# A constant second operand in PSUM for the scans of stick-breaking attention, two score banks instead of three, carries kept in the scan buffers, fused state and gate operations, reversed operand allocation and transfers in program order, in a one-core hybrid decoder layer

## The chip, the cores and the metric

The kernel runs on one core of one Trainium2 chip. The metric is the time of one launch on the device, in microseconds. The engines are TensorE (PE, its weight loads as PEld), VectorE (DVE), ScalarE (ACT), GpSimd (POOL) and SyncE (SP), which issues nearly all transfers.

## The reference

One decoder layer over 2048 tokens of width 1024, all in float32. The input is normalised and projected once; the columns feed three mixers that run side by side. Their outputs are normalised per head (two of them with a swish gate), joined, projected and added to the input. A SwiGLU feed-forward network of width 2816 with its own norm follows. Cut to what matters here:

```python
z = einsum('bhqd,bhkd->bhqk', qb, kb) * scale
log_keep = where(mask, log_sigmoid(-z), 0.0)
log_rest = cumsum(log_keep, axis=3, reverse=True) - log_keep
weights = exp(where(mask, log_sigmoid(z) + log_rest, -inf))
o_b = einsum('bhqk,bhkd->bhqd', weights, vb)          # stick-breaking attention, 6 heads of 64
state = dec * state + k_to_end.T @ v                  # GLA (4 heads) and HGRN2 (4 heads), per chunk
mixed = concat([rms(o_a) * silu(g), rms(o_b), rms(o_c) * silu(h)])
x = x + mixed @ w_out
gate, up = split(rms_norm(x) @ w_ffn_up)
x = x + (silu(gate) * up) @ w_ffn_down
```

The weight of a key is its sigmoid times the product of (1 - sigmoid) over the keys between it and the query.

## The kernel before

**Number format and products.** Every large product is done in three matmuls of a float32r type: an operand is split into a rounded high part and the remainder as a low part (`conv_w`, L247: a copy on ACT, L248, and a subtraction on POOL or DVE, L249), and high x high, high x low and low x high are summed. The input projection, the up-projection and the down-projection are cut into two by two blocks and done with seven products instead of eight (numbered 1 to 7; sums of blocks are their operands, and each result is added to several output blocks).

**Stages.** The order of the program is: input projection; attention and the two recurrences, interleaved; the output projection, which begins inside the attention; the up-projection; the down-projection. A scheduler puts the instructions of each engine in order from a simulated timeline at build time, as their operands come free there. Where the kernel wants an order of its own it says so: in the attention the class `Chain` ties every PE instruction behind the one written before it, and `tc.keep_in_program_order` ties an instruction behind the one written before it on its engine.

**Attention (`z_step`, L959, to `a_step`, L1010).** Work goes in slots: a unit is a pair of head and key block of 512 for a query group of 512, with four slots (blocks of 128 queries). A slot computes z on PE, one sigmoid of -z into `kp` (L990) and one of z into `w` (L991) on ACT, and then on DVE a running product over `kp`, read backwards (L993, the scan; its second operand is not used, the operation being a bypass, and is given as `kp` again). The last value, the carry, is copied to a small tile by POOL (L996) and is the start of the same block's scan two units later. The product of `w` with the scan's result is made on DVE for one block in four (two in four for the first query group) and on POOL otherwise (L997). Five slots later `w` is transposed on PE (`t_step`), and seven slots later multiplied with the values. The scan's results take turns in a pool of two buffers.

**Recurrences (`decay_levels`, L1050; `hg_chunk`, L1133; `gla_chunk`, L1196).** Between the attention's steps, in the same PE chain, stand steps of the two gated recurrences, in 16 chunks of 128 tokens, two chunks open at a time. A step is a level: POOL and DVE scale queries and keys, PE makes scores into a score tile of one PSUM bank (pool `c_pss`, three banks), and DVE or ACT reads it into a masked matrix (L1075, L1103). A chunk has ten score tiles for HGRN2 and eleven for GLA; the last chunk leaves out two of each. At its end the state is multiplied by the decay on POOL (L1192, L1247) and the new term in PSUM is added on DVE (L1193, L1248).

**Output projection (`Out`, L804).** It takes over the recurrences' PSUM banks when these are done, while the attention goes on. For each of 16 row tiles `load` fetches the mixers' output and the gates, makes 14 squares with sums (one per head, ACT, L826), a reciprocal root in small DVE operations, a scaling of three segments (DVE, L834) and three products with gates and gains (POOL, L836 to L839). `turn` transposes the tile in two halves into a single PSUM bank (pool `d_pt`) and splits them; the steps then run 48 matmuls, the residual, the second norm, and `left`, two more transposes of halves of the row tile before through the same bank. `left_sums` builds the operands of the up-projection and stores them to `xs_s`.

**Up-projection (`up`, L1380; `left_in`, L1369).** The seven left operands of half the tokens stay in SBUF (pool `e_h`, on the right side, 14 tiles of 8 KB per partition, allocated in the order 1, 5, 6, 2, 3, 7, 4, from low addresses to high); they arrive through two staging buffers. The right side held the output weights `woh`, `wol` and `gffn` at its outer end, and the tiles of the output projection below them. Each of 22 column tiles runs seven products, gates the result and stores `h` to `hs_s` (L1418).

**Down-projection (from L1443).** For each of the seven products in the order 1, 2, 5, 6, 3, 7, 4, eight row tiles fill the eight PSUM banks over 11 k-steps of 24 matmuls. A k-step's left operand (`left_dn`, L1460) is made of transfers `ar` and `xa` of `hs_s` (512 KB each, L1454), its right operand (`right_dn`, L1487) of transfers `br` and `xb` of the weights (256 KB each, L1458). `xa` and `xb` of product 5 stay in SBUF and are changed in place for products 6, 3 and 4. `flush_dn` (L1517) adds a product's eight banks to the sums `acc`, which hold the residual; they are fetched in sixteen transfers after the third k-step of the first product (L1558, tied to program order). After products 2, 3, 7 and 4 a quarter of the result is stored (L1544).

## Time and profile before

| | us |
|---|---|
| median of three runs | 3147.08 |
| lowest and highest | 3138.09, 3147.41 |
| profiled execution | 3147.62 |
| its span, first to last instruction | 3145.8 |
| PE busy | 2831.5 |
| DVE busy | 2116.2 |
| POOL busy | 1639.2 |
| ACT busy | 1344.4 |

The profile is one execution of the program. A stage is read in three steps: what share of it each engine is busy (the windows), what PE waited for in it (the waits, summed by who ended them), and then single instructions in order of time (the timeline), where the number in brackets is the idle time of the engine just before, and the name behind it the one that ended it. A busy PE is not a PE at its peak, since the ends of matmuls are modelled: in a steady stretch one of 512 columns starts every 0.23 us, while its own length reads 0.39 us. The granted clock of TensorE is a share of full speed.

### The profile page before, as it was taken

How to read it: one execution, taken by the hardware profiler on the slowest of the kernel's cores; microseconds unless marked ns; L12 is line 12 of the kernel's file. 1: busy time of each engine (PE TensorE's matmuls, PEld its weight loads, DVE VectorE, ACT ScalarE, POOL GpSimd, SP SyncE). 2: the span in 40 equal slices, each digit the busy share in tenths (PEclk: the TensorE clock that was granted, in tenths of full speed). 3: DMA queues.
4: the chain of work that ended last, by engine and by line, in shares of the span. 5: the costliest groups of instructions: out<-in, count | busy, mean ns of one | idle time of the engine just before them, and what ended most of it. 6: DMA issues, size and time to landing. Idle time of an engine off the chain costs nothing. (4 is left out here: it accounts for less than half of the span.)

```text
span 3145.8 us, 43879 instructions
## 1 busy us (share of the span) xinstructions
PE 2831.5 (90%) x14882; PEld 2309.9 (73%) x14882; DVE 2116.2 (67%) x3508; ACT 1344.4 (43%) x2834; POOL 1639.2 (52%) x1640
## 2 busy tenths in 40 slices
PE   5898999997888889878888799999999997899998
PEld 5897878996666666655666588888788885677776
DVE  8886665886888888988866455555755553267443
ACT  5554534453555555566644333333433332323222
POOL 5342554344787887854633244444544442257635
PEclk9999999998889998989988899999999998999999
DMA  3534432536533333123354332222422225564173
GB/s 116 159 108 134 139 127 97 136 94 166 153 104 107 98 100 93 58 94 108 130 173 161 134 114 85 87 87 84 142 87 81 81 81 216 212 234 144 64 241 131
DMA packets 346095, 389.82 MB, mean 124 GB/s; under 512 B 59152, under 2 KB 258064, under 8 KB 344080
## 3 DMA queue, kind: packets, MB, share of 16 engines
q1 hardware_dynamic: 341776, 381.77, 38.4%
q0 software_dynamic: 4096, 5.25, 0.5%
q8 instruction: 119, 1.95, 0.3%
q14 instruction: 104, 0.85, 0.1%
HBM read 278.93 MB, written 108.00 MB: 123 GB/s over the span
## 5 line engine op out<-in xcount | busy, mean ns | idle before, releaser
L1390 PE MATMUL gu<-ah,uh 128*128 128x512 f32 x1232 | 481.3, 391 | 10.1 <-ACT ah L248 10.1
L1391 PE MATMUL gu<-al,uh 128*128 128x512 f32 x1232 | 481.8, 391 | 6.0 <-DVE al L249 5.9
L1392 PE MATMUL gu<-ah,ul 128*128 128x512 f32 x1232 | 481.0, 390 | 0.0
L249 POOL TENSOR_TENSOR ul<-bs,uh 128x512 fp32r<-128x512 f32 x176 | 241.6, 1374 | 243.2 <-ACT uh L248 243.2
L249 POOL TENSOR_TENSOR ul<-us,uh 128x512 fp32r<-128x512 f32 x132 | 176.6, 1339 | 203.6 <-ACT uh L248 203.6
L1390 PEld LDWEIGHTS gu<-ah,uh 128*128 128x128 f32 x1232 | 232.3, 189 | 60.3 <-ACT ah L248 12.0
L1391 PEld LDWEIGHTS gu<-al,uh 128*128 128x128 f32 x1232 | 232.5, 189 | 56.9 <-DVE al L249 8.7
L1552 PE MATMUL dn<-dbh,dah 128*128 128x512 f32 x616 | 224.6, 402 | 48.4 <-ACT dbh L248 41.8
L1392 PEld LDWEIGHTS gu<-ah,ul 128*128 128x128 f32 x1232 | 232.3, 189 | 48.1
L245 DVE TENSOR_TENSOR h<-h,gu 128x512 f32<-128x512 f32 x176 | 120.9, 687 | 205.3 <-PE gu L1392 123.5
L1553 PE MATMUL dn<-dbl,dah 128*128 128x512 f32 x616 | 243.9, 396 | 12.7 <-POOL dbl L249 12.6
L1554 PE MATMUL dn<-dbh,dal 128*128 128x512 f32 x616 | 242.4, 395 | 3.1 <-DVE dal L249 3.0
L248 ACT ACTIVATE uh<-bs 128x512 fp32r<-128x512 f32 x176 | 110.9, 632 | 299.8 <-PE gu L1391 299.6
L993 DVE TENSOR_TENSOR_SCAN pr<-kp,ca 128x513 f32<-128x513 f32 x144 | 213.2, 1484 | 22.0 <-ACT kp L990 17.7
L997 POOL TENSOR_TENSOR w<-w,pr 128x512 f32<-128x512 f32 (+1 forms) x174 | 191.8, 1102 | 46.0 <-DVE pr L993 26.0
L990 ACT ACTIVATE kp<-z 128x512 f32<-128x512 f32 (+1 forms) x240 | 128.0, 533 | 183.4 <-PE z L104 168.7
L104 PE MATMUL z<-sk,sq 128*128 128x512 f32 (+1 forms) x480 | 170.7, 440 | 14.5 <-ACT w L991 8.1
L107 PE MATMUL wt<-ident,w 128*128 128x128 f32 x816 | 147.9, 294 | 39.2 <-POOL w L997 34.3
L1552 PEld LDWEIGHTS dn<-dbh,dah 128*128 128x128 f32 x616 | 118.4, 194 | 80.5 <-ACT dbh L248 49.3
L249 DVE TENSOR_TENSOR dal<-ar,dah 128x1024 fp32r<-128x1024 f32 x44 | 65.0, 1485 | 163.1 <-ACT dah L248 163.0
L248 ACT ACTIVATE uh<-us 128x512 fp32r<-128x512 f32 x132 | 83.1, 631 | 193.0 <-PE gu L1391 130.6
L104 PEld LDWEIGHTS z<-sk,sq 128*128 128x128 f32 x480 | 80.7, 208 | 104.7 <-issue 37.9
(385 smaller groups left out, 7845.1 us busy)
## 6 DMA issues: line engine op xcount, KB each, us to landing
us<-in_w_ffn_up SPq DMA_DIRECT2D x88, 512.0 KB, 3.8
ar<-hs_s SPq DMA_DIRECT2D x88, 512.0 KB, 4.0
hs_s<-h SPq DMA_DIRECT2D x44, 512.0 KB, 2.6
br<-in_w_ffn_down SPq DMA_DIRECT2D x88, 256.0 KB, 3.2
sk<-sk_s SPq DMA_DIRECT2D x60, 256.0 KB, 2.9
st<-xs_s SPq DMA_DIRECT2D x14, 1024.0 KB, 5.2
xt<-in_x SPq DMA_DIRECT2D x24, 512.0 KB, 4.8
sq<-sq_s SPq DMA_DIRECT2D x48, 256.0 KB, 4.8
```

Source lines behind the costliest of these rows:

```text
L104: self._add(nc.tensor.matmul(*a, **k))
L107: self._add(nc.tensor.transpose(*a, **k))
L248: act.activation(wh, st, AF.Copy)
L249: eng.tensor_tensor(wl, st, wh.bitcast(F32), op=ALU.subtract)
L993: dve.tensor_tensor_scan(pr[:, n::-1], kr, kr, 1.0 if u.diag else u.carry[b], op0=ALU.mult, op1=ALU.bypass)
L997: (dve if (b in DVE_B0 if g == 0 else b == DVE_B) else pool).tensor_tensor(w, w, pr[:, 1:n + 1], op=ALU.mult)
L1390: pe.matmul(pv, bh[:, k, :], ah[:, :, k, :], start=(k == 0), stop=False)
L1391: pe.matmul(pv, bh[:, k, :], al[:, :, k, :], start=False, stop=False)
L1392: pe.matmul(pv, bl[:, k, :], ah[:, :, k, :], start=False, stop=(k == KH - 1))
L1552: pe.matmul(pss[i], ah[:, ts_], bh, start=(k == 0), stop=False)
L1553: pe.matmul(pss[i], ah[:, ts_], bl, start=False, stop=False)
L1554: pe.matmul(pss[i], al[:, ts_], bh, start=False, stop=(k == NK - 1))
```

## The change

- **Scan.** `ones`, a column of ones in a PSUM bank of its own, takes the place of the second operand, broadcast along the row, as long as the recurrences run; afterwards the bank goes to the output projection and the scan is given `kp` twice as before. The scores get two banks instead of three.
- **Carries.** Two fixed scan buffers (`prs`, 529 columns) take the place of the pool. Each unit writes one or two columns further right, so that its last value stays untouched until it is read as the start of a later scan. The POOL copies go.
- **States.** The decay product and the add become one fused operation per head (four) or head pair (two) on DVE.
- **Output projection.** One square of the whole row tile on ACT and three reductions on DVE in place of 14 squares with sums; 14 fused products (scale and gate in one) on DVE in place of three on DVE and three on POOL. Once the attention is over, transposes take turns in three PSUM banks instead of one.
- **Up-projection.** The left operands of the first half are allocated in the reverse order, 4, 7, 3, 2, 6, 5, 1.
- **Down-projection.** Every load of `hs_s` and of the weights is tied to program order. The right operand's tiles move to the right side, with a third raw buffer. The order of products becomes 1, 5, 6, 2, 3, 7, 4. After products 5 and 7 both sums are added on DVE straight from PSUM, without the copy on ACT. Two of the three sums of product 6 are put off: two of these POOL adds follow each later k-step.

```diff
@@ class Out
+            self.ptx = None
+        def pt_tile(self, name):
+            return (self.ptx or self.pt).tile([P, KH, P], F32, tag="pt", name=name)
...
+            sq = self.wk.tile([P, D], F32, tag="sq", name=f"msq{t}", bufs=1)
+            act.activation(sq, m, AF.Square)
             for a, b, w, i, j in segs:
-                for h in range(j - i):
-                    sj = self.sm.tile([P, GDV], BF16, tag="sj", name=f"sj{t}_{i}_{h}", bufs=1)
-                    act.activation(sj[:, :w], m[:, a + h * w:a + (h + 1) * w], AF.Square,
-                                   accum_out=ms[:, i + h:i + h + 1])
+                dve.tensor_reduce(ms[:, i:j], sq[:, a:b].rearrange("p (h d) -> p h d", d=w),
+                                  axis=AX.X, op=ALU.add)
...
-                mv = m[:, a:b].rearrange("p (h d) -> p h d", d=w)
-                dve.tensor_tensor(mv, mv, rs[:, i:j].unsqueeze(2).to_broadcast([P, j - i, w]),
-                                  op=ALU.mult)
-            pool.tensor_tensor(m[:, 0:384], m[:, 0:384], gt[:, 0:384], op=ALU.mult)
-            pool.tensor_tensor(m[:, 768:], m[:, 768:], gt[:, 384:], op=ALU.mult)
-            mv = m[:, 384:768].rearrange("p (h d) -> p h d", d=SD)
-            pool.tensor_tensor(mv, mv, gs64.unsqueeze(1).to_broadcast([P, SH, SD]), op=ALU.mult)
+                for n in range(i, j):
+                    cs = slice(a + (n - i) * w, a + (n - i + 1) * w)
+                    g_ = gt[:, cs] if a == 0 else gs64 if a == 384 else \
+                        gt[:, 384 + (n - i) * w:384 + (n - i + 1) * w]
+                    dve.scalar_tensor_tensor(m[:, cs], m[:, cs], rs[:, n:n + 1], g_,
+                                             op0=ALU.mult, op1=ALU.mult)
@@ attention
-        ps_s = open_pool(prc, "c_pss", 3, PSUM)
+        ps_s = open_pool(prc, "c_pss", 2, PSUM)
+        ps_1 = open_pool(prc, "c_ps1", 1, PSUM)
+        ones = [ps_1.tile([P, 512], F32, name="one")[:, 0:1]]
+        dve.memset(ones[0], 1.0)
...
+        prs = [sbk.tile([P, 513 + 16], F32, name=f"pr{i}", bufs=1) for i in range(2)]
...
-                    u.carry = [sbk.tile([P, 1], F32, tag=f"ca{i}", name=f"ca{h}_{g}_{i}", bufs=4)
-                               for i in range(4)]
+                    u.carry = [1.0] * 4
...
-                    u.q, u.carry = p.q, p.carry
+                    u.q, u.carry = p.q, p.last
+                u.last = []
...
-            pr = sbk.tile([P, 513], F32, tag="pr", name=f"pr{h}_{g}_{c}_{b}")
+            at = 4 * (g - c) + 2 * u.j + b // 2
+            pr = prs[b % 2][:, at:at + 513]
...
-            dve.tensor_tensor_scan(pr[:, n::-1], kr, kr, 1.0 if u.diag else u.carry[b],
-                                   op0=ALU.mult, op1=ALU.bypass)
-            if c > 0:
-                pool.tensor_copy(u.carry[b], pr[:, 0:1])
+            dve.tensor_tensor_scan(pr[:, n::-1], kr,
+                                   ones[0].to_broadcast([P, n + 1]) if ones else kr,
+                                   u.carry[b], op0=ALU.mult, op1=ALU.bypass)
+            u.last.append(pr[:, 0:1])
@@ hg_chunk (gla_chunk alike, two operations)
-            pool.tensor_tensor(s_new, s_old, dec.to_broadcast([P, HH, HDV]), op=ALU.mult)
-            dve.tensor_tensor(s_new, s_new, pu, op=ALU.add)
+            for i in range(HH):
+                dve.scalar_tensor_tensor(s_new[:, i, :], s_old[:, i, :], dec[:, i, :], pu[:, i, :],
+                                         op0=ALU.mult, op1=ALU.add)
@@ when the recurrences are done
                 prc.close()
+                ones.clear()
                 out_.open()
@@ after the attention
+    ptx = ExitStack()
+    out_.ptx = open_pool(ptx, "d_px", 3, PSUM)
     for t in outs:
         pass
+    ptx.close()
@@ up-projection
+    ops = {m: tuple(hp.tile([P, 4, KH, P], F32R, tag=f"{x}{m}", name=f"{x}{m}_0")
+                    for x in ("ah", "al")) for m in ORDER[::-1]}
@@ down-projection
+    bop = open_pool(pd, "g_bo", 3, side="right")
...
-        dma.dma_start(t_, hs_s[kh * NK + k][j].rearrange("p i j t -> p (i j t)"))
+        tc.keep_in_program_order(
+            dma.dma_start(t_, hs_s[kh * NK + k][j].rearrange("p i j t -> p (i j t)")))
...
-        dma.dma_start(t_, w_dn[r:r + P, j * 512:j * 512 + 512])
+        tc.keep_in_program_order(dma.dma_start(t_, w_dn[r:r + P, j * 512:j * 512 + 512]))
...
-            t_ = rop.tile([P, 512], F32, tag="br", name=f"br{nm}_{kh}{j}")
+            t_ = bop.tile([P, 512], F32, tag="br", name=f"br{nm}_{kh}{j}")
...
         elif m in (5, 7):
             c = {5: c12, 7: c21}[m]
-            tmp = rop.tile([P, 512], F32, tag="tmp", name=f"tmp{m}_{i}")
-            act.activation(tmp, ps, AF.Copy)
             add(c, c, ps)
-            add(c22, c22, tmp, pool)
+            add(c22, c22, ps)
+            if m == 7:
+                done(8 + i, 1)
         elif m == 6:
             u = held[i]
             add(u, u, ps)
-            add(c12, c12, u, pool)
             add(c21, c21, u)
-            add(c22, c22, u, pool)
+            later.append(lambda: add(c12, c12, u, pool))
+            later.append(lambda: add(c22, c22, u, pool))
...
-    for m in (1, 2, 5, 6, 3, 7, 4):
+    for m in (1, 5, 6, 2, 3, 7, 4):
...
+            for fn in later[:2]:
+                fn()
+            del later[:2]
```

## Rows read from the trace of the kernel before

**Rows 1.** Windows by stage: start and length, busy us and instructions per engine, clock, DMA.

```profile
755.00:1592.00 837.00, 723.44 (x4746) 535.09 (x4747) 700.60 (x1164) 478.20 (x1269) 601.55 (x847) 0.91 0.38 110
1592.00:1785.00 193.00, 148.87 (x642) 116.35 (x641) 112.49 (x316) 72.62 (x267) 59.91 (x51) 0.86 0.48 157
1785.00:2639.00 854.00, 845.50 (x3696) 696.23 (x3696) 509.30 (x594) 293.39 (x463) 409.79 (x302) 0.99 0.29 95
2639.00:3145.80 506.80, 438.27 (x1849) 352.52 (x1848) 240.49 (x187) 136.10 (x179) 251.07 (x153) 0.94 0.53 186
```

**Rows 2.** Waits of PE, 755 to 1592: us in total, times, longest.

```profile
PE wt L107 <- POOL w L997: 34.3, 27, 3.9
...
PE mt L107 <- POOL m L836: 8.8, 1, 8.8
```

**Rows 3.** Groups of the page: count, busy us, mean ns, idle before.

```profile
L993 DVE TENSOR_TENSOR_SCAN pr<-kp,ca 128x513 f32<-128x513 f32 x144 | 213.2, 1484 | 22.0 <-ACT kp L990 17.7 <-POOL w L997 1.7 <-ACT sj L826 1.1
...
L996 POOL COPY ca<-pr 128x1 f32<-128x1 f32 x144 | 45.1, 314 | 85.3 <-DVE pr L993 56.6 <-DVE rfy L84 9.2 <-DVE rmy L84 4.5
```

**Rows 4.** The tile pr: shortest, median and longest in ns.

```profile
L993 DVE TENSOR_TENSOR_SCAN pr<-kp,ca x144: 1247/1286/2356, 856.2 to 1569.7; 128x513 f32<-128x513 f32 x144
...
L997 DVE TENSOR_TENSOR w<-w,pr x66: 267/686/1779, 756.5 to 1558.5; 128x512 f32<-128x512 f32 x36, 128x128 f32<-128x128 f32 x24, 128x384 f32<-128x384 f32 x6
```

**Rows 5.** A group of the page, an add with an operand in PSUM.

```profile
L245 DVE TENSOR_TENSOR h<-h,gu 128x512 f32<-128x512 f32 x176 | 120.9, 687 | 205.3 <-PE gu L1392 123.5 <-issue 81.8
```

**Rows 6.** Waits of PE, 1592 to 1795.

```profile
PE po L902 <- ACT mh L89: 12.9, 9, 4.1
```

**Rows 7.** Windows of line 826 alone, 1592 to 1785: busy us of ACT.

```profile
1592.00:1785.00 193.00, 34.90 (x196) 0.86 0.48 157
```

**Rows 8.** Timeline: start, us, instruction; two score tiles and two readings before them.

```profile
794.00 1.10 PE L104 MATMUL sch<-hq,hk 128*64 128x64 f32 x8
794.84 0.72 DVE L1075 COPY_PREDICATED st_h<-masks,sch 128x256 f32<-128x256 int8 x1
...
1376.64 0.68 PE L104 MATMUL scg<-qx_g,gk 128*128 128x128 f32 x4 [0.97 <-DVE qx_g L1071]
1377.61 0.32 DVE L1248 TENSOR_TENSOR s_g<-s_g,gpu 128x192 f32<-128x192 f32 x1
```

**Rows 9.** Timeline of PE, end of the output projection.

```profile
1768.06 0.39 PE L904 MATMUL po<-woh,ml 128*128 128x512 f32 x1
...
1784.79 0.79 PE L1390 MATMUL gu<-ah,uh 128*128 128x512 f32 x1 [7.53 <-ACT ah L248]
```

**Rows 10.** Timeline of ACT, the same stretch.

```profile
1784.11 4.08 ACT L248 ACTIVATE ah<-st 128x512 fp32r<-128x512 f32 x6 [6.21 <-DMA xs_s<-xs]
```

**Rows 11.** Timeline of PE, start of the down-projection.

```profile
2638.62 0.39 PE L1392 MATMUL gu<-ah,ul 128*128 128x512 f32 x1
2662.54 3.44 PE L1552 MATMUL dn<-dbh,dah 128*128 128x512 f32 x8 [23.53 <-ACT dbh L248]
...
2693.27 3.43 PE L1552 MATMUL dn<-dbh,dah 128*128 128x512 f32 x8 [12.75 <-ACT dbh L248]
```

**Rows 12.** Timeline of SP's queue, the same stretch.

```profile
2641.15 0.32 SPq L1418 DMA_DIRECT2D hs_s<-h  x1
...
2652.19 1.62 SPq L1458 DMA_DIRECT2D br<-in_w_ffn_down  x2
...
2665.94 15.97 SPq L1558 DMA_DIRECT2D acc<-x_s  x16
2682.92 0.33 SPq L1458 DMA_DIRECT2D br<-in_w_ffn_down  x1
```

**Rows 13.** DMA issues of the page: count, KB each, median us to landing.

```profile
ar<-hs_s SPq DMA_DIRECT2D x88, 512.0 KB, 4.0
```

**Rows 14.** Timeline of SP's queue at the turn from product 2 to 5.

```profile
2789.17 1.46 SPq L1454 DMA_DIRECT2D ar<-hs_s  x2
...
2800.80 0.42 SPq L1544 DMA_DIRECT2D out<-acc  x1
```

46 lines of the change are left out of this document (26 added, 20 removed).

## The prediction

> **What bounds the kernel now.** I read the windows by stage first [rows 1]: the 3145.8 us span has five stages, and TensorE (PE) is the engine that should never stand still. In the up-projection (1785 to 2639) it issues 3696 matmuls in 854 us, 0.231 us each, busy 845.5 us: nothing is to be had there. The other stages are not like that. Attention with the recurrences (755 to 1592) leaves PE idle 113.6 of 837 us, the rest of the output projection (1592 to 1785) 44.1 of 193, the down-projection 68.5 of 506.8. Next I read who ends PE's waits. In the attention the first is the product w on POOL, 34.3 us, and one wait of 8.8 us for the first row tile of the output projection [rows 2]. In the tail of the output projection it is the split on ACT, 12.9 us [rows 6], and at its end PE waits 7.5 us more for the first operand of the up-projection [rows 9]. The down-projection loses 23.5 us before its first matmul and 12.8 us three k-steps later [rows 11].
>
> The profiled execution took 3147.62 us, 1.8 us more than its span and 0.5 us from the median of the three runs (3147.08). The sum is made against 3147.6. A difference under 0.3% (9.4 us) is no change here.
>
> **A. Attention, 755 to 1592.** Removed: 144 carry copies on POOL, 45.1 us by their row [rows 3]; two state products per chunk on POOL. The scan of 513 elements has a mean of 1484 ns [rows 3] but a minimum of 1247 and a median of 1286 [rows 4]; the excess sits in a few slow ones (maximum 2356), as if something held them. With the second operand in PSUM I take the minimum: 144 x 0.237 = 34 us of DVE in a stage where DVE is busy 700.6 and POOL 601.6 of 837 us [rows 1]. Scans that run after the recurrences close still take two operands from SBUF, so this is an upper bound, and 0 the lower. That the PSUM operand costs nothing is read from the nearest row: an add of 512 columns with one operand in PSUM takes 687 ns [rows 5], one with both in SBUF a median of 686 [rows 4].
>
> [...]
>
> Added on DVE: six fused state operations per chunk in place of two adds (15 chunks, four more of about 0.27 us, the minimum of a two-operand product [rows 4]: +16 us) and the heavier row-tile preparation, counted in B. So DVE ends about 18 us lighter, POOL over 45 us lighter. PE's waits for POOL should halve (34.3 to 17), and the 8.8 us wait for the first row tile shrinks by 6, since its squares and POOL products are shortened. That is -23, and another -8 for the smaller POOL and DVE waits.
>
> Against it stands the lost third score bank. The trace has 332 score tiles (21 per chunk, 16 chunks, 4 missing at the end). With two banks a tile must wait until the one two before is read out. I compared each tile's start with that moment: 73 start too early for two banks, by 60 us in all; the first and the last [rows 8]: the scores at 794.00 start before the predicated copy at 794.84 is done at 795.56, and those at 1376.64 before the state add is done at 1377.93. What is queued behind such a wait is PE's whole hand-ordered chain: the next z, transposes and products. A lower bound is 0 (DVE reads out faster), an upper 60 or more. I take a quarter, +15, because a delayed PE also delays the tiles behind it, which opens the next gap. A = -23 - 8 + 15 = **-16** (-70 to +45). The carry now stays on DVE, so no scan waits for POOL; the two scan buffers still make each scan wait for the product two slots earlier, as two pool buffers did.
>
> **B. Tail of the output projection.** The 14 squares per row tile keep ACT busy 34.9 us in this stage [rows 7]; one square replaces them. Three reductions and 14 fused products come onto DVE, about 17 x 0.27 = 4.6 us a row tile, and three products each leave DVE and POOL. DVE has room: 112.5 of 193 us [rows 1]. Three transpose banks in place of one let transposes go ahead of the split that empties them. [...]
>
> **C. Start of the up-projection.** The last matmul of the output projection starts at 1768.06, the first of the up-projection at 1784.79 [rows 9]. The operand's conversion on ACT waited for the transfer xs_s out of the staging tile [rows 10]: operand 1 is laid where that tile was. The operands fill 112 KB of the right side and the output weights its outer 68 KB; allocated in reverse, operands 1, 5 and 6 lie over the weights, free with the last matmul. Conversion and subtraction of a quarter cost under 2 us, so the start can be near 1771. The supply of further operands keeps its two staging buffers. **-12** (-16 to 0).
>
> **D. Start of the down-projection.** SP's own rows show the reason for the two stalls [rows 12]: after the last store of h (2641.15) come transfers for later products, the first br issues only at 2652.19, then sixteen acc loads from 2665.94, and the br of the fourth k-step at 2682.92. With program order, ar and br of three k-steps are queued right behind that store, then acc, then the fourth. First matmul: 2641.5 + 4.0 for landing [rows 13] + 0.7 for a conversion (4.08/6 [rows 10]) = 2646.2. Three k-steps of 24 matmuls last 16.6 us, 1.6 more at the slow clock (3.44 us for the first eight [rows 11]): 2664.4. The fourth waits for acc: from its first issue to the restart took 27.3 us (2665.94 to 2693.27); behind six loads, about 2644.5, that gives 2671.8. Before, the fourth started at 2693.27: -21.5. The loads of product 5, which were fetched early, now come within its own stage; I leave 2.5 us for that: **-19** (-25 to -8).
>
> **E. Rest of the down-projection.** The other 32 us of idle time there partly go: POOL's sixteen adds after product 6 are spread over later steps, and the right operand has a third buffer. I take 22 of the 32. But the order has a price. Before, loads of the next product pass the stores of out: ar issued at 2789.17, the first out of that turn at 2800.80 [rows 14]. Now each load is queued behind the last store of the product before, which waits for its add. After products 2 and 3 that is 0.7 (add) + 0.4 (issue) + 4.0 (landing) + 0.7 (conversion) = 5.8 us of empty PE each; after product 7, with two adds per bank on DVE, 8 x 0.69 = 5.5 more: 11.3. Together 23 us. **+1** (-15 to +20).
>
> **Sum.** -16 - 22 - 12 - 19 + 1 = -68: 3147.6 - 68 = 3080 us.
>
> **Rivals.** *Slower: two score banks decide.* Without the 15 us for banks the sum is -83, so from 83/332 = 0.25 us per score tile on, the kernel is slower. If each tile costs 0.35 us (116 us), it takes 3147.6 - 83 + 116 = 3181. For it: PE's order is fixed, and 73 pairs are short already. Against it: 259 are not, and DVE gets lighter. Chance 0.10. *The port is freed in full.* If the slow scans come from POOL reading SBUF at the same time, POOL's operations are held by scans as well, and PE's waits for it go whole: 34.3 and 8.8 [rows 2], twice the 8 us of smaller ones, and nothing for the banks make A -60 and the time 3036. Chance 0.14. [...] The spread of the scan [rows 4] agrees; how much of it reaches PE no row shows. *Order costs more than it gives.* If stores hold the next product's loads at every turn and A gives nothing, D and E cancel: 3147.6 - 22 - 12 = 3114, or 3130 with B at its low end. Chance 0.10. *Nothing reaches the path:* the waits removed are replaced by the next in line, 3147. Chance 0.06.
>
> **Numbers.** The forecast has 0.60 and its own range 3045 to 3115. From 3030 to 3132 all but about 2 in 10 is held: outside lie the slower case, the no-change case and the far end of the freed port (0.10 + 0.06 + 0.03). Faster by over 0.3%: 0.60 + 0.14 + 0.10 = 0.84; within: 0.06; slower: 0.10.
>
> **What would show it.** Right: scans near 1250 ns with little spread until the recurrences end; no carry copies; PE's wait for w about 17 us; up-projection starting some 3 us after the last po; first dn about 5 us after the last store of h; new PE gaps of about 6 us after products 2 and 3 and 11 after 7. Wrong: a scan over 1350 ns with the PSUM operand, score matmuls waiting for predicated copies in most chunks, a first dn behind acc as before, or an idle DVE with PE still waiting for POOL.

## The result and the profile after

| | before | changed |
|---|---|---|
| median of the runs | 3145.18 us (4 runs, 3138.09 to 3147.41) | 3122.27 us (4 runs, 3120.13 to 3129.18) |
| ratio, 95% interval | | 0.9937 (0.992 to 0.9954) |
| profiled execution | 3147.62 us, span 3145.8 | 3122.30 us, span 3120.5 |

The change makes the kernel faster, by 0.6%. That is inside the range of 3030 to 3132 us, but it is 42 us short of the 3080 us forecast: the direction was right, the size a third of what was expected.

The windows by stage of the changed kernel, with the columns of [rows 1]:

```profile
752.00:1579.00 827.00, 718.81 (x4734) 529.65 (x4735) 685.30 (x1345) 448.03 (x1022) 429.94 (x646) 0.92 0.38 111
1579.00:1762.00 183.00, 143.81 (x654) 115.55 (x652) 126.30 (x417) 46.42 (x79) 35.42 (x27) 0.89 0.49 160
1762.00:2622.00 860.00, 848.64 (x3695) 696.41 (x3696) 516.36 (x594) 293.89 (x464) 414.69 (x306) 0.99 0.29 96
2622.00:3120.50 498.50, 435.24 (x1851) 354.67 (x1849) 252.76 (x203) 127.80 (x163) 235.95 (x137) 0.94 0.53 188
```

POOL lost 172 us of work in the attention (601.6 to 429.9) and ACT 26 us in the rest of the output projection (72.6 to 46.4), yet these two stages are only 10 us shorter each. The up-projection is 6 us longer.

For a sharper cut I use the starts of first and last matmuls, which every profile has: the first score product z, the last transpose of w, the last matmul of the output projection (po), the first and last of the up-projection (gu) and of the down-projection (dn). The stretches between them, in us, from starts rounded to 0.1 us (all kernels below are explained in the next section):

| kernel | z to last w | to last po | to first gu | to last gu | to first dn | to last dn |
|---|---|---|---|---|---|---|
| before | 827.1 | 186.2 | 16.7 | 853.8 | 23.9 | 478.7 |
| changed | 819.7 | 181.3 | 9.3 | 860.0 | 3.3 | 490.5 |
| e1 attention undone | 830.2 | 181.5 | 9.3 | 860.5 | 3.3 | 498.6 |
| e2 row tile undone | 819.8 | 164.9 | 9.3 | 861.0 | 3.3 | 493.0 |
| e3 one transpose bank | 810.3 | 190.2 | 10.4 | 859.1 | 3.2 | 491.7 |
| e4 stores later, acc spread | 814.9 | 181.6 | 9.3 | 859.2 | 3.3 | 443.1 |
| e5 products as before | 821.9 | 161.0 | 9.3 | 858.8 | 3.3 | 498.4 |
| e6 stores later | 804.6 | 181.5 | 9.3 | 860.0 | 3.3 | 455.0 |
| e7 old places | 811.5 | 181.0 | 9.3 | 860.2 | 3.3 | 490.1 |
| e8 before, two banks | 838.7 | 183.7 | 16.8 | 855.4 | 24.4 | 479.7 |
| e9 three banks, no constant | 821.1 | 182.3 | 9.3 | 860.3 | 3.2 | 496.3 |
| e10 old places, no square tile | 811.6 | 168.6 | 16.0 | 854.3 | 3.3 | 492.8 |
| e11 e5 and e4 together | 816.1 | 164.3 | 9.3 | 860.4 | 3.3 | 442.0 |
| e12 e11, w on POOL | 829.9 | 163.4 | 9.3 | 862.9 | 3.3 | 444.1 |
| e13 row tiles one earlier | 815.8 | 181.7 | 9.3 | 859.8 | 3.3 | 492.6 |
| e14 e11, adds later | 814.9 | 164.2 | 9.3 | 860.2 | 3.3 | 445.4 |
| e15 e14, first row tile later | 802.0 | 173.8 | 9.5 | 863.2 | 3.3 | 443.3 |
| e16 block sums on DVE | 803.1 | 159.6 | 9.5 | 856.0 | 3.3 | 495.1 |
| e17 all, fused products | 796.2 | 167.8 | 9.4 | 857.5 | 3.3 | 444.9 |
| e18 all, products as before | 803.8 | 159.6 | 9.4 | 859.1 | 3.3 | 445.7 |

The changed kernel, e3, e4, e6 and e7 have the same attention code, and their first column runs from 804.6 to 819.7: one profile tells that stage to some 8 us only. The tail in the second column lies within 1.3 us in the seven kernels that have the changed kernel's output projection (181.0 to 182.3: the changed one, e1, e4, e6, e7, e9, e13). Other kernels with equal tails are up to 3.7 us apart (the kernel before and e8; e2 and e10; e5, e11, e12 and e14). In e15, e17 and e18 the tail holds 516 of the 768 matmuls of the output projection, in all others 498, so the tails of these three compare with each other only.

The scans in the view of the tile pr (duration in ns as min/median/max) did what was forecast:

```profile
L1001 DVE TENSOR_TENSOR_SCAN pr<-kp,pr,one x105: 1243/1271/1283, 845.5 to 1384.2; 128x513 f32<-128x513 f32 x105
L1001 DVE TENSOR_TENSOR_SCAN pr<-kp,pr x39: 1258/1279/2110, 1386.4 to 1555.3; 128x513 f32<-128x513 f32 x39
```

With the constant in PSUM not one of 105 scans takes over 1283 ns; with both operands in SBUF, after the recurrences have closed, the maximum is 2110 again, as it was 2356 before [rows 4]. What the slow ones meet can be counted in the trace, over all scans of 513 elements. With the constant, 106 of 127 run while a POOL instruction runs, and none is slow. With both operands in SBUF, 30 of 41 run with no POOL instruction beside them and none takes over 1289 ns; the other 11 have a median of 2028.

PE's waits for w on POOL fell from 34.3 us [rows 2] to 14.0; the wait for the first row tile is as long as before, only on DVE now. New are waits for the readings of score tiles (st_h, st_g) and for the state operations (s_h, s_g) on DVE. From the view of waits, 752 to 1579 us:

```profile
PE wt L107 <- POOL w L1008: 14.0, 14, 5.5
PE mt L107 <- DVE m L840: 9.3, 1, 9.3
PE ho L104 <- DVE st_h L1086: 8.6, 3, 3.2
PE sch L104 <- DVE s_h L1204: 5.6, 5, 1.7
PE sch L104 <- DVE st_h L1086: 5.2, 5, 1.7
```

The same view of the kernel before, 755 to 1592 us, has two rows that belong beside them, its largest wait for POOL after w and its largest of the new kind:

```profile
PE sch L104 <- POOL hk L1117: 11.5, 10, 5.1
PE go L104 <- DVE st_g L1075: 3.3, 2, 2.0
```

Summed over all such rows from the first z to the last w, PE's waits that POOL ended fell from 71.9 us to 16.3, and those that score readings and state operations on DVE ended rose from 7.8 to 44.0. All waits together fell only from 119.5 to 113.0.

In the tail of the output projection PE now stands still rarely and long, where it stood often and briefly: 12 times for 32.4 us in all, before 26 times for 30.4 us. ACT ended 21.3 us of these waits before and ends 11.5 now; DVE ended 6.2 us and ends 21.0 now. These are single rows of PE's timeline:

```profile
1603.16 0.79 PE L904 MATMUL po<-woh,mh 128*128 128x512 f32 x1 [8.98 <-ACT mh L89]
1643.81 0.80 PE L906 MATMUL po<-woh,ml 128*128 128x512 f32 x1 [4.01 <-DVE ml L90]
1678.61 0.80 PE L904 MATMUL po<-woh,mh 128*128 128x512 f32 x1 [6.35 <-DVE xt L909]
1712.94 0.79 PE L906 MATMUL po<-woh,ml 128*128 128x512 f32 x1 [5.76 <-DVE ml L90]
```

In the down-projection the 23.5 us before the first matmul are gone [rows 11], the stall three k-steps later is not, and three new ones follow products 2, 3 and 7:

```profile
2625.47 2.12 PE L1574 MATMUL dn<-dbh,dah 128*128 128x512 f32 x8 [2.91 <-ACT dbh L248]
2655.40 3.56 PE L1574 MATMUL dn<-dbh,dah 128*128 128x512 f32 x8 [13.21 <-ACT dbh L248]
2906.36 3.78 PE L1574 MATMUL dn<-dbh,dah 128*128 128x512 f32 x8 [8.33 <-ACT dah L248]
2979.10 2.50 PE L1574 MATMUL dn<-dbh,dah 128*128 128x512 f32 x5 [10.37 <-ACT dbh L248]
3054.78 3.55 PE L1574 MATMUL dn<-dbh,dah 128*128 128x512 f32 x8 [13.24 <-ACT dbh L248]
```

SP's own rows (start, duration, issue) show both causes, against [rows 12, 14]: the first loads stand ahead of the last store of h, all sixteen acc loads stand between the third and the fourth k-step, and the loads after product 2 stand behind eight stores of out:

```profile
2611.49 0.32 SPq L1476 DMA_DIRECT2D ar<-hs_s  x1
2614.21 0.33 SPq L1480 DMA_DIRECT2D br<-in_w_ffn_down  x1
2624.70 0.32 SPq L1436 DMA_DIRECT2D hs_s<-h  x1
2626.44 16.04 SPq L1580 DMA_DIRECT2D acc<-x_s  x16
2643.48 0.32 SPq L1476 DMA_DIRECT2D ar<-hs_s  x1
2894.02 5.09 SPq L1541 DMA_DIRECT2D out<-acc  x8
2899.21 0.41 SPq L1476 DMA_DIRECT2D ar<-hs_s  x1
```

### The profile page after: what moved, and what is told of

It is laid out like the page before. It is cut to its first block, busy times and chain, and to the rows that moved or that the text cites. A ratio compares the mean times of both kernels' runs of the same rounds, so it can differ in the third digit from the quotient of the medians.

```text
span 3120.5 us, 43531 instructions
## 1 busy us (share of the span) xinstructions
PE 2817.2 (90%) x14882; PEld 2301.0 (74%) x14882; DVE 2136.6 (68%) x3809; ACT 1280.5 (41%) x2386; POOL 1431.7 (46%) x1402
## 4 chain that ended last, share of the span: by engine, by line
PE 54%; DVE 16%; DMA 7%; issue 5%; POOL 2%; ACT 2%; SPq 1%; DVEq 0%; POOLq 0%; ACTq 0%
PE gu L1409 9%; PE gu L1410 9%; PE gu L1408 9%; PE dn L1574 3%; PE dn L1575 3%; PE dn L1576 3%; PE z L104 2%; PE av L104 2%; DVE pr L1001 2%; PE wt L107 2%; PE sch L104 2%; DMA br<-in_w_ffn_down 2%; DVE m L840 1%; PE scg L104 1%; PE ho L104 1%
## 5 line engine op out<-in xcount | busy, mean ns | idle before, releaser
L1574 PE MATMUL dn<-dbh,dah 128*128 128x512 f32 x616 | 231.3, 404 | 52.2 <-ACT dbh L248 39.7
L1001 DVE TENSOR_TENSOR_SCAN pr<-kp,pr,one 128x513 f32<-128x513 f32 x105 | 133.6, 1273 | 21.0 <-ACT kp L997 20.6
```

What stands on the lines that cost most here:

```text
L1001: dve.tensor_tensor_scan(pr[:, n::-1], kr, ones[0].to_broadcast([P, n + 1]) if ones else kr, u.carry[b], op0=ALU.mult, op1=ALU.bypass)
L1574: pe.matmul(pss[i], ah[:, ts_], bh, start=(k == 0), stop=False)
```

## Experiments

Ratios are to the kernel before, with 95% intervals, timed on the same chip. The changed kernel's is 0.9937.

### Attention: what the constant, the banks and POOL's relief are worth

**e1.** `ps_s` with three banks, `tensor_tensor_scan(pr, kr, kr, ...)`, carry copies and state products on POOL as in the kernel before; the rest is the changed kernel.

> The changed kernel with its attention part undone: both scan operands from SBUF again, three score banks, carry copies and state products on POOL; all other parts of the change stay. In the profile of the changed kernel the stretch from the first score product z to the first matmul of the output projection that has no attention beside it took 827.3 us, against 834.7 us before. Theory 1 (the attention part gives only that: PE's waits for POOL became waits for DVE, which does the state products now): about 3122 + 7 = 3129 us, scans with a mean near 1480 ns again, PE's waits for w on POOL near 34 us. Theory 2 (the DVE work that the attention part added also made the row tiles late, so that the part gives nothing or costs): 3115 to 3122 us, and a shorter tail of the output projection than the 173 us of the changed kernel. Theory 3 (the part gave the 16 us of the forecast and another part took them back): 3138 us.

Measured: 3142.28 us, 0.9975 (0.9963 to 0.9987). By the ratios the part is worth 0.9975 - 0.9937 = 0.4%, 12 us: between theories 1 and 3. The tail stays at 181.5 us, so theory 2 is out.

**e8.** The kernel before with one edit:

```diff
-        ps_s = open_pool(prc, "c_pss", 3, PSUM)
+        ps_s = open_pool(prc, "c_pss", 2, PSUM)
```

> The kernel before with two score banks in place of three and nothing else changed. Theory 1 (a quarter of what the pairs that start too early lack): 15 us slower than the kernel before, ratio 1.005, PE's waits for the predicated copies and the state products on DVE grow by that. Theory 2 (two banks decide): 60 us or more slower, ratio 1.02. Theory 3 (DVE reads out in time whatever the banks): no difference, ratio within 0.002 of 1.

Measured: 3160.91 us, 1.004 (1.0026 to 1.0055), 13 us. Theory 1. PE's waits for score readings and state operations on DVE grow by more than that, from 7.8 to 37.0 us, while its waits for POOL fall from 71.9 to 57.6.

**e9.** The changed kernel with `c_pss` at 3, without `ones`, and the scan reading `kr` twice; carries and fused state products as changed.

> The changed kernel with three score banks and both scan operands from SBUF; the scan buffers that hold the carries, the fused state products and everything else stay. Two banks alone cost the kernel before 0.4% (13 us), and the attention part as a whole gave 0.4% (12 us), so that the rest of the part must give about 25 us. Theory 1 (the constant in PSUM gives most of these 25, because scans no longer meet POOL): without it and with the bank back the time is 5 to 15 us longer than the changed kernel's, ratio 0.996 to 0.998, and the mean of the 513-element scan is back above 1400 ns. Theory 2 (the carry copies and state products taken from POOL give most of them, and the scan's 0.2 us each is hidden): the time is 5 to 12 us shorter, ratio 0.990 to 0.992.

Measured: 3129.52 us, 0.9941 (0.9921 to 0.9962), the changed kernel's ratio within the intervals: neither theory. The long scans are back at a mean of 1421 ns (view of lines, kept apart by shape), and PE's wait for w is 26.0 us:

```profile
L998 DVE TENSOR_TENSOR_SCAN pr<-kp,pr 128x513 f32<-128x513 f32 x144 | 204.4, 1421 | 12.0 <-ACT kp L994 9.7 <-POOL w L1004 2.1
```
```profile
PE wt L107 <- POOL w L1004: 26.0, 25, 5.0
```

So the constant and the bank that it takes cancel, to within the some 8 us that the intervals leave. The waits show both sides: all of PE's waits for POOL are 39.4 us here and 16.3 in the changed kernel, those for score readings and state operations on DVE 7.1 here and 44.0 there. What is left of the part, e1 against e9, 0.0034 or 11 us, goes with the carries and the state products; these two were not parted.

**e12.** e11 (below), with `DVE_B = -1` and `DVE_B0 = (0,)`: nearly all products w on POOL.

> The run before (gate products as before, stores later, acc spread) with the quarter of the products w that DVE does in the attention moved to POOL (of the first group, one of its two). In the changed kernel these 56 products took 40.8 us of DVE up to 1400 us, and POOL was busy 430 of 827 us. Theory 1 (DVE is now what PE waits for in the attention): 5 to 15 us shorter than the run beside it. Theory 2 (a product takes 1.12 us on POOL and 0.73 on DVE and PE waits for w on POOL again): 5 us or more longer.

Measured: 3074.29 us, 0.9762 (0.9749 to 0.9774) against 0.9715 for e11: 15 us longer. The result fits theory 2, its reason doesn't: PE's waits for w on POOL are 17.2 us, 19.0 in e11. PE's busy time grew for the same matmuls, at a lower granted clock (first row e12, second e11; windows from the first z to the last w):

```profile
756.30:1586.20 829.90, 722.14 (x4699) 532.16 (x4700) 663.24 (x1184) 447.93 (x1019) 515.71 (x730) 0.90 0.38 110
```
```profile
750.30:1566.40 816.10, 706.44 (x4701) 519.76 (x4701) 679.47 (x1245) 445.91 (x1019) 462.72 (x672) 0.93 0.39 111
```

Why the clock was granted lower here stays open.

### Output projection: why 22 us became 5

**e2.** Fourteen squares on ACT and products in two steps as before; three transpose banks stay.

> The changed kernel with the preparation of a row tile undone: 14 squares on ACT in place of one, no reductions, three products on DVE and three on POOL in place of fourteen fused ones on DVE; the three transpose banks stay. Theory 1 (the fourteen fused products, 30 us of DVE in the tail, stand in DVE's queue ahead of the adds and splits that PE waits for, and cost about what the one square gives): 3119 to 3125 us; PE's waits in the tail for DVE shrink and those for ACT grow. Theory 2 (the forecast: the squares were what held PE): 3135 us or more, the tail from the first to the last matmul of the output projection 10 us or more longer than 173 us.

Measured: 3110.4 us, 0.9859 (0.9833 to 0.9885): undoing this part makes the kernel 0.8% faster, more than either theory allowed. The tail falls to 164.9 us, with the waits that DVE ends down from 21.0 to 9.8 us.

**e3.** Without `out_.ptx = open_pool(ptx, "d_px", 3, PSUM)`.

> The changed kernel with one transpose bank in the tail of the output projection in place of three. In the profile of the kernel before, PE had 16 waits of 0.7 to 1.2 us in front of transposes in the tail; in that of the changed kernel there are none of them. Theory 1 (the third and second bank removed those): 16 x 0.75 = 12 us slower, 3134 us, and the short waits are back. Theory 2 (the row tiles are late on DVE anyway, so the short waits come out of the long ones): 3122 to 3125 us, short waits back and the waits of 4 to 9 us shorter by as much.

Measured: 3134.4 us, 0.9944 (0.9924 to 0.9964), no difference that the runs can tell; the tail is 190.2 us, 9 longer, as theory 1 has it. Tails together: with one bank 186.2 and 183.7 (row tiles as before: the kernel before, e8) and 190.2 (changed), with three 164.9 and 168.6 (as before: e2, e10) and 181.3 (changed). With row tiles as before the banks alone are worth 15 to 21 us there, nearly all that was forecast for the whole term; the new preparation takes 13 to 16 of them back.

**e5.** Only the fourteen products undone; the one square and the reductions stay:

```diff
-                for n in range(i, j):
...
-                    dve.scalar_tensor_tensor(m[:, cs], m[:, cs], rs[:, n:n + 1], g_, ...)
...
+                dve.tensor_tensor(mv, mv, rs[:, i:j]..., op=ALU.mult)
+            pool.tensor_tensor(m[:, 0:384], m[:, 0:384], gt[:, 0:384], op=ALU.mult)
...
```

> The changed kernel with the fourteen fused products of a row tile undone (three products on DVE and three on POOL, as before), but the one square and its three reductions kept. With squares and products both as before, the ratio to the kernel before was 0.986 against 0.994 with both changed, and the tail from the last transpose of w to the last matmul of the output projection took 164.9 us against 181.3. Theory 1 (the fused products in DVE's queue are the cost): ratio 0.986 or less, the tail 165 us or shorter, because ACT is relieved as well. Theory 2 (the one square with its reductions, a chain from ACT to DVE that ends later than fourteen sums written by ACT alone, is the cost): ratio 0.992 to 0.994, the tail 175 us or more.

Measured: 3107.12 us, 0.9871 (0.985 to 0.9891), tail 161.0 us: theory 1. The square with its reductions is no worse than fourteen squares (164.9). The fused products cost 17 to 20 us of tail (e11, e12 and e14, with the same tail, have 163.4 to 164.3), and the waits that DVE ends fall to 4.0 us without them.

**e13.** To tell DVE's load from the order, the preparation of a row tile was issued one tile earlier (`prep(t + 2)` beside `load(t + 1)`).

> The changed kernel with the preparation of a row tile (loads, square, reductions, the fourteen fused products on DVE) issued one row tile earlier in the program; its work is the same. In the changed kernel the tail from the last transpose of w to the last matmul of the output projection takes 181 us with the fused products and 161 us without them. Theory 1 (not the load on DVE but the place of the products just ahead of the adds and splits that PE waits for): the tail 170 us or less, ratio 0.990 or less. Theory 2 (the load on DVE): the tail 178 us or more, ratio as for the changed kernel, 0.994.

Measured: 3123.27 us, 0.9928 (0.9908 to 0.9948), tail 181.7 us. This reads as theory 2 but is no test: DVE's timeline shows the products at nearly the same places, and PE's five long waits are the same (9.58, 3.54, 4.01, 6.34 and 5.78 us for 8.98, 3.23, 4.01, 6.35 and 5.76). The order on an engine is not that of the program's text where nothing pins it.

What the trace does show is where the products are slow. POOL's and then DVE's timeline of the changed kernel ahead of the 6.35 us wait (start, duration; xn are n in a row):

```profile
1670.58 1.27 POOL L242 TENSOR_TENSOR xs<-xa,xa 128x512 f32<-128x512 f32 x1 [28.75 <-ACT xa L871]
1671.93 1.26 POOL L245 TENSOR_TENSOR xa<-xa,xa 128x512 f32<-128x512 f32 x1
1673.27 1.39 POOL L242 TENSOR_TENSOR xs<-xa,xa 128x512 f32<-128x512 f32 x1
1674.73 1.39 POOL L242 TENSOR_TENSOR xs<-xa,xs 128x512 f32<-128x512 f32 x1
```
```profile
1654.24 0.17 DVE L84 SCALAR_TENSOR_TENSOR rmy<-rma,rmy 128x14 f32<-128x14 f32 x1
1655.08 1.00 DVE L840 SCALAR_TENSOR_TENSOR m<-m,rmy,gt 128x96 f32<-128x96 f32 x4
...
1670.59 1.29 DVE L84 SCALAR_TENSOR_TENSOR rmy<-rma,rmy 128x14 f32<-128x14 f32 x1
1671.91 3.08 DVE L840 SCALAR_TENSOR_TENSOR m<-m,rmy,gt 128x96 f32<-128x96 f32 x4
1674.92 2.26 DVE L840 SCALAR_TENSOR_TENSOR m<-m,rmy,gs 128x64 f32<-128x64 f32 x6
1677.88 0.68 DVE L909 TENSOR_TENSOR xt<-xt,po 128x512 f32<-128x512 f32 x1
```

An operation of 14 columns that takes 0.17 us at 1654 takes 1.29 at 1670, when POOL has just begun a block sum, and it ends with that sum. Four products that take 1.00 us at 1655 take 3.08. The add of po, for which PE waits, stands behind them. This is no single case: of the 224 fused products in the trace 194 run with no POOL instruction beside them and none takes over 0.32 us; the 30 that do run beside one have a median of 1.07 us.

**e16.** The four block sums of every second row tile go to DVE:

```diff
-            sub(s3, a11, a21, pool)
-            add(a21, a21, a22, pool)
-            sub(s2, a21, a11, pool)
-            sub(s4, a12, s2, pool)
+            sub(s3, a11, a21, dve)
...
```

> The changed kernel with the four block sums of every second row tile in the output projection on DVE instead of POOL; the fourteen fused products stay on DVE. Theory 1 (POOL's sums hold the fused products, each for the rest of a POOL instruction): although DVE gets 4 x 0.7 us more per two row tiles, PE's waits of 3.2, 4.0, 6.4 and 5.8 us in the tail shrink and the tail from the last transpose of w to the last matmul of the output projection falls from 181 to 170 us or less; ratio 0.991 or less. Theory 2 (DVE has too much to do or in the wrong order): the tail stays at 181 us or grows; ratio 0.994 or more.

Measured: 3088.93 us, 0.9802 (0.9778 to 0.9826), by the ratios 42 us less than the changed kernel (33 by the medians as they stand); the tail is 159.6 us with DVE no lighter. Theory 1, and more than it asked. Of the gain 22 us lie in the tail. The largest other difference between the two profiles, 16.6 us, is in the attention, which one profile tells to some 8 us only. The waits that DVE ends in the tail fall from 21.0 to 6.2 us. DVE's products fall from means of 382 and 349 ns (changed kernel, 1579 to 1762 us) to 298 and 280 (e16, 1556 to 1720 us), and PE's granted clock in the tail rises from 0.90 to 0.97. The view of lines of the changed kernel and of e16, then the windows of the tail of e16 and of the changed kernel:

```profile
L840 DVE SCALAR_TENSOR_TENSOR m<-m,rmy,gt 128x96 f32<-128x96 f32 (+1 forms) x56 | 18.3, 382 | 0.2
L840 DVE SCALAR_TENSOR_TENSOR m<-m,rmy,gs 128x64 f32<-128x64 f32 x42 | 11.8, 349 | 0.0
```
```profile
L840 DVE SCALAR_TENSOR_TENSOR m<-m,rmy,gt 128x96 f32<-128x96 f32 (+1 forms) x64 | 15.3, 298 | 0.1
L840 DVE SCALAR_TENSOR_TENSOR m<-m,rmy,gs 128x64 f32<-128x64 f32 x48 | 10.5, 280 | 0.0
```
```profile
1556.00:1722.00 166.00, 145.99 (x697) 115.18 (x695) 122.12 (x447) 47.62 (x81) 7.91 (x6) 0.97 0.56 182
```
```profile
1571.60:1753.00 181.40, 148.97 (x681) 118.57 (x679) 123.32 (x405) 44.92 (x77) 34.26 (x26) 0.90 0.50 162
```

The sums themselves are also shorter on DVE, 0.69 us against 1.3; e16 doesn't separate that from the holding. How much DVE is held can be estimated from the traces: for each of its operations that overlaps a POOL instruction in the tail, take its time less the median of the same operation with none beside it (over the kernels here), and sum what is over 0.1 us. That gives 29.7 us on 40 operations in the kernel before, 26.6 on 32 in e5, 20.5 on 21 in the changed kernel and 4.6 on 5 in e16. So the fused products did not make the holding more frequent. They changed what is held: before, 19 of the 40 lay in the preparation of a row tile (norm of the heads and products) and 19 in the second norm; in the changed kernel 20 of the 21 lie in the preparation, like those ahead of the add shown above.

### The start of the up-projection

**e7.** The changed kernel without the reversed `ops`.

> The changed kernel with the operands of the up-projection laid out as before. In the changed kernel the first matmul of the up-projection starts 9.3 us after the last of the output projection (16.7 before), but the stage then takes 860 us (854 before): PE runs at its full rate from 41.3 us after the last matmul of the output projection on, before from 43.7. Theory 1 (the supply of the seven operands through two staging buffers and the conversions on ACT and DVE sets the time, not the first one): the first matmul 7 us later, the last matmul of the up-projection at most 3 us later counted from the last of the output projection. Theory 2 (the early start is a gain of its own): both 7 us later or more.

Measured: 3117.24 us (one run); first gu 9.3 us after the last po, stage 860.2 us: nothing changes, neither theory. The edit that I gave the 12 us is idle here.

**e10.** e7 and e2 together, so also without the 4 KB tile of the squares.

> The changed kernel with the row tile's preparation as before (so without the new buffer of 4 KB for the squares) and the operands of the up-projection laid out as before. Either of the two edits alone left the first matmul of the up-projection 9.3 us after the last of the output projection. Theory 1 (either edit moves the first operand off the staging tile of the last transfer): now the 16.7 us of the kernel before are back. Theory 2 (the gap went with the transpose banks or the earlier row tiles): 9 to 11 us again.

Measured: 3107.33 us (one run), 16.0 us: theory 1. The first gu waits for the operand again:

```profile
1750.74 0.80 PE L1408 MATMUL gu<-ah,uh 128*128 128x512 f32 x1 [7.98 <-ACT ah L248]
```
```profile
1750.06 2.19 ACT L248 ACTIVATE ah<-st 128x512 fp32r<-128x512 f32 x4 [6.66 <-DMA xs_s<-xs]
```
```profile
1757.00 0.80 PE L1407 MATMUL gu<-ah,uh 128*128 128x512 f32 x1 [1.21 <-ACT ah L248]
```

(the first two rows are e10's, the third e7's). In e10 the conversion waits for the transfer out of the staging tile again, as in [rows 10]. So either edit moves the first operand off that tile: the reversed places, or the new tile, which I take to shift the staging tiles by its 4 KB. And it is worth nothing: from the last po to the last gu e10 takes 16.0 + 854.3 = 870.3 us, e2 with the early start 9.3 + 861.0 = 870.3.

### Down-projection: what stands behind the stores

**e4.** Two edits (`done` now only collects the stores, `stores()` issues them):

```diff
-            if m == 1 and k == 2:
-                for t in range(NT):
+            if (m == 1 and k >= 1) or (m == 5 and k < 6):
+                for t in [len(acc)]:
...
+            if k == 2:
+                stores()
```

> The changed kernel with two edits in the down-projection: the stores of out are issued after the loads of the third k-step of the next product instead of ahead of that product's loads, and the sixteen acc loads are issued one per k-step (ten in the first product, six in the second) instead of all sixteen after the third k-step. In the profile of the changed kernel PE stands still 13.2 us before the fourth k-step, 8.3 us after product 2, 10.4 us after product 3 and 13.2 us after product 7, together 45.1 us. Theory 1 (loads queued behind stores and behind acc are the whole of these stalls): 3122 - 45 = 3077 us, at the least 3087 us. Theory 2 (the transfers themselves are the limit, so that the loads would be late in any order): 3110 to 3120 us, with the waits spread over the k-steps.

Measured: 3071.86 us, 0.9747 (0.9726 to 0.9768): theory 1. The first to the last dn takes 443.1 us in place of 490.5, 47.4 less; of the stalls over 3.2 us on PE's timeline only one for POOL is left:

```profile
2830.21 0.80 PE L1583 MATMUL dn<-dbl,dah 128*128 128x512 f32 x1 [6.04 <-POOL dbl L249]
```

**e6.** The stores alone.

> The changed kernel with the stores of out issued after the loads of the third k-step of the next product; the sixteen acc loads stay together after the third k-step. With both edits the down-projection from its first matmul took 444.2 us against 491.6, the ratio was 0.975. Theory 1 (each stall belongs to its own queue): the stalls of 8.3, 10.4 and 13.2 us after products 2, 3 and 7 go and the 13.2 us before the fourth k-step stays: from the first matmul 491.6 - 31.9 = 460 us, the ratio near 0.983. Theory 2 (the loads behind acc hold all the later ones up, so that the stalls share a cause): the acc stall takes more than 13.2 us with it, and this run gives less than half of the 47 us, 470 us or more.

Measured: 3080.42 us, 0.9792 (0.9768 to 0.9816); 455.0 us, 35.5 less; the stall before the fourth k-step stays (12.91 us). Theory 1: each stall has its own cause in the queue.

**e14.** e11 (below) with POOL's adds after product 6 from `k >= 2` on.

> The run with gate products as before, stores later and acc spread (ratio 0.9715), and in it the sixteen POOL adds after product 6 start at the third k-step of the next product instead of the first. There PE waited 6.0 and 2.5 us for dbl on POOL in the third and fourth k-steps after product 6, as it waited 6.0 us in the kernel before. Theory 1 (POOL's first adds wait for the sums on DVE, and the next right operand is queued behind them): both waits go, 8 us less, ratio 0.969. Theory 2 (the operand is late by its transfer): waits and ratio stay.

Measured: 3060.89 us, 0.9731 (0.9712 to 0.9749), the wait still 6.03 us. As in e13 the edit moved next to nothing. POOL's timeline shows nine adds in one go ahead of the operand, where the changed kernel's has eight in 14.74 us, although its text spreads them two per k-step. POOL's rows, then one of DVE's:

```profile
2793.20 16.55 POOL L245 TENSOR_TENSOR acc<-acc,u 128x512 f32<-128x512 f32 x9
2809.71 2.24 POOL L249 TENSOR_TENSOR dbl<-br,dbh 128x512 fp32r<-128x512 f32 x1
```
```profile
2799.55 6.88 DVE L245 TENSOR_TENSOR acc<-acc,u 128x512 f32<-128x512 f32 x4
```

### Together

**e11.** The changed kernel with the edits of e5 and e4.

> The changed kernel with three edits: gate products of a row tile on DVE and POOL as before, out stores issued after the loads of the third k-step of the next product, acc loads one per k-step. The first alone had the ratio 0.987, the other two together 0.975, the changed kernel 0.994. Theory 1 (different stages, so they add): 0.994 - 0.007 - 0.019 = 0.968, about 3046 us. Theory 2 (the gain of the products is given back by the row tiles' stores or the up-projection): 0.974 or more.

Measured: 3059.29 us, 0.9715 (0.9697 to 0.9733): nearer theory 1 than theory 2. It is 0.0035, 11 us, short of the sum of the parts, which the intervals of the parts leave open.

**e15.** e14 with `OUT_LEAD = 8`.

> The run with the POOL adds later, and in it the first transposes of the output projection come eight slots after its first loads instead of five. PE waits 8.8 us for the first row tile in the kernel before, 9.3 us in the changed one. Theory 1 (attention work fills the wait): 9 us less than the run beside it, ratio 0.003 lower. Theory 2 (the row tiles then come later and the tail grows by what the wait gave): no difference.

Measured: 3054.78 us, 0.9706 (0.9687 to 0.9725), not told apart from e14. The wait is still there (10.97 us), and the tail grew from 164.2 to 173.8 us, with 18 more matmuls of the output projection in it, while the stretch before shrank from 814.9 to 802.0: theory 2 for the most part.

**e17, e18.** Block sums on DVE, stores later, acc spread, `OUT_LEAD = 8`; e17 with fused products, e18 with the products as before.

> The changed kernel with the block sums on DVE, eight slots before the first row tile, stores later and acc spread; fused products kept. With the gate products as before and the sums on POOL the ratio of this combination was 0.9706. Theory 1 (POOL's sums were what made the fused products dear): 0.971 or less. Theory 2 (the products as before are better in any case): 0.975 or more.

> The same with the gate products on DVE and POOL as before, block sums on DVE. Theory 1: the three large products on DVE meet POOL's gate products rather than its sums, little changes against the 0.9706 with the sums on POOL, 0.968 to 0.972. Theory 2 (DVE's load decides): 0.974 or more.

Measured: e17 3039.3 us, 0.965 (0.9624 to 0.9676); e18 3031.05 us, 0.9628 (0.9604 to 0.9653), the fastest kernel of the study, 91 us below the changed one by the medians. e17 lies where its theory 1 has it. e18 lies below the range of both of its theories: taking the sums off POOL gains with the products as before too, 0.9706 to 0.9628 and 173.8 to 159.6 us of tail against e15. The intervals of e17 and e18 overlap, but e17's tail is 8.2 us longer (167.8), although its held time by the estimate above is the smaller one (4.5 us against 10.4). So with the sums off POOL the fused products are cheaper than the 17 to 20 us of before, not free, and what is left is not holding.

## Why the prediction was wrong in size

Against its own terms, by the profiles of before and after: attention -16 forecast, -7.4 measured; tail -22, -4.9; start of the up-projection -12, 9.3 - 16.7 + 860.0 - 853.8 = -1.2; start of the down-projection -19, -21.4 (23.9 to 3.3 us, and 29.9 for the first three k-steps with their stall against 30.7); the rest of it +1, +12.6. With 2.9 us ahead of the attention these make the 25.2 us between the spans (25.3).

**A, attention: the sum held, its two sides did not.** By e1 the part is worth 12 us; the five profiles of the same code have a mean of 812.2 us, 15 less than the one of the kernel before. But PE's waits for POOL fell by 55.6 us (71.9 to 16.3; 8.8 of them, the first row tile's, only moved to DVE), where the sum had 31 for all of its gains. And the waits for score readings and state operations on DVE rose by 36.2 us, in 39 waits over 16 chunks, where it had 15; the prediction had named score matmuls waiting for predicated copies as a sign of being wrong. That the two misses cancel is luck. The 13 us of e8 do not contradict the 36: in the kernel before waits on POOL shrank by 14.3 us meanwhile. Wrong too was that the first row tile's wait shrinks by 6: it went from 8.8 to 9.3 us. The scan's PSUM operand costs nothing that shows (minimum 1243 ns against 1247). The 686 ns that the prediction set beside the add is the median of a product over three widths; of these, the four of 512 columns with no POOL instruction beside them took 678 to 692 ns, so the reading stands.

**B, tail: the step "DVE has room: 112.5 of 193 us" failed.** The 22 us that the sum has for B, 5 at the low end, were the author's estimate: 15 us of PE's idle time and 7 for its granted clock. No run shows the 7 us: the clock of the stage went from 0.86 [rows 1] to 0.89 in the changed kernel. By its busy share DVE still had room in the changed kernel (126.3 of 183 us). But PE waits for single operations, and a busy share says nothing of when they come. The waits that ACT ended fell by 9.8 us, as meant; those that DVE ended rose by 14.8 (6.2 to 21.0), so that PE's idle time, instead of losing 15 us, grew by 2.0. That the tail is 4.9 us shorter all the same comes from PE's busy stretches; which part of the change did that, no run shows. The waits for DVE took two things together: fused products ahead of the adds and splits that PE waits for, and POOL's block sums, which hold operations of that preparation. Without the first (e5) the waits that DVE ends are 4.0 us, without the second (e16) 6.2. How the 17 to 20 us of tail share out between holding and the longer work on DVE stays open; e17 against e18 puts 8 on the products where almost nothing is held. I had the holding in hand as the second rival, priced it for scans and for POOL, and did not apply it to operations that the change adds. The trace shows the holding (0.17 to 1.29 us for an operation of 14 columns), and e16 turns the tail's 181 us into 160.

**C: the step "operand 1 is laid where that tile was" was right for the kernel before, but the term took the start of a stage for its gain.** The start itself came 7.4 us earlier, not 12: "near 1771" left out that PE still has the last row tile's transposes to do, which wait for its norm on DVE. In the changed kernel they begin 6.1 us after the last po (1752.90), and the first gu at 1762.18 waits only 1.20 us more:

```profile
1759.04 1.94 PE L869 MATMUL xt<-ident,xt 128*128 128x128 f32 x8 [5.73 <-DVE xt L862]
```

And I wrote that the supply of further operands keeps its two staging buffers and gave that no price. It was the bound: PE waits for al and ah until 1794.23 us in the changed kernel, 41 us after the last po, until 1811.88 before, 44 after.

**D: right,** by 2 us, but by luck in its parts: the first loads need only parts of h that were stored early, so program order puts them ahead of the last store, and the first dn comes 3.3 us after the last gu, where the sum had 7.6 (2646.2 against 2638.62). The sixteen acc loads kept their 13 us, where it had 7.4 (2664.4 to 2671.8). With k-steps a little quicker than assumed, the fourth started 33.2 us after the last gu, as the sum had it.

**E: right in kind, mis-sized.** The stalls behind the stores were forecast at 5.8, 5.8 and 11.3 us, 23 in all, and measured 8.3, 10.4 and 13.2, 31.9. The landing was taken from the median of all 88 loads of the kernel before (4.0 us, [rows 13]); behind the eight stores after product 2 a load's median is 5.1 us, and the 5.09 us for issuing eight stores came on top. The other waits of PE's timeline in that stretch fell by 16.5 (27.6 to 11.1), not 22: the sixteen adds on POOL were not spread, and the 6.0 us wait behind them is in both kernels. e4 shows that the whole of the price was avoidable.

Of the rivals "order costs more than it gives" named the right place, but D outweighed E. "Two score banks decide" fell with e8. "The port is freed in full" came near for the waits on POOL (71.9 to 16.3 us), but not in time, because it gave nothing for the banks.

## What to carry to other kernels

Pinning loads to program order also pins them behind every store that stands ahead: move the stores, or spread what isn't needed yet, in the same edit (47 us here). Before work moves to an engine with room, look at what stands behind it there and what the neighbouring engine runs at that moment: the fourteen small products lost no more time beside POOL than DVE had lost before (20.5 us against 29.7 by the estimate above), but PE now waited for what stood behind them. A part that removes one engine's waits is worth only what the next wait in line leaves: here 56 us of waits for POOL against 36 for a bank. And the start of a stage is a gain only if its second and third inputs come as early as its first.

## What the runs showed of the hardware

How much a running POOL operation can cost a small Vector operation with two SBUF inputs: 128x14 went from 0.17 to 1.29 us, fused products from at most 0.32 us alone to a median of 1.07 beside POOL, and in e14's down-projection four adds of 512 columns with both inputs in SBUF took 6.88 us beside POOL's nine, 1.7 each against 0.69 for the sums on DVE. A scan of 513 elements with one operand in PSUM was not slowed once in the 106 cases that ran beside POOL (maximum 1283 ns). And in e16's tail, where stalls went, the granted clock rose too, from 0.90 to 0.97: 681 matmuls kept PE busy 149.0 us in the changed kernel's tail, 697 took 146.0 us in e16's. The opposite case, e12, where the clock was 0.90 against 0.93 in e11 with PE's waits for w on POOL no longer (17.2 us against 19.0), is unexplained.
